# Attention scores: two rows of queries take their blocks of keys in turn

## The chip, the cores and the metric

The kernel runs on one core of a Trainium2 chip. The metric is the device time of one execution in microseconds (us), lower is better. The core has a matrix engine (TensorE, in the rows PE for the matmuls and PEld for the loading of their weights), VectorE (DVE), ScalarE (ACT), GpSimd (POOL) and SyncE (SP), which only issues transfers here. Each engine works through its own instructions in the order in which they were written and waits on semaphores for the others.

## The reference, cut to what matters

One step of a streaming encoder with two layers, for a prompt of 2048 tokens and 8 running streams of 16 tokens. Each layer projects its input to all branches, runs attention A (8 heads of 64, each chunk of 64 tokens sees itself and the 8 chunks before it, with a learned bias), a gated convolution B, and attention C (4 heads with two maps of 32 dimensions, all chunks up to the own one), and projects back. Per head:

```
A:  p = softmax(q k^T / 8 + bias)                      # at most 9 chunks of keys
    out = p v
C:  p1 = softmax(q1 k1^T / sqrt(32)), p2 = softmax(q2 k2^T / sqrt(32))
    out = (p1 - lambda * p2) v                         # two maps, the whole past
```

## The kernel before

The 2048 tokens go through in four segments of 512 (`s` = 0 to 3) for each of the two layers (`l`), which makes eight rounds. Each round is a list of units in `ORDER`, written as letters: P is the projection of a C head and C its attention, K the projection of an A head and A its attention, V, G and O are value, gate and output projections, B the convolution, T a piece of the running streams' attention, N the norm for the next round. Layer 1's last segment has a list of its own.

The functions don't issue instructions, they add them to a `Program`. Its `order` then plays the whole program on five engines with a cost for each instruction and a latency for each pair of engines (`LATENCY`; 127 ns from VectorE to VectorE), and at each step starts the ready instruction that stands earliest in the program. Matmuls of the projections are put back by `LATER` = 350 places, so that they fill what the attention leaves free. The list that comes out is issued as it stands, so that every engine's order is fixed before the kernel runs. Buffers are handed out under a name in the program's order: PSUM bank pair `s` (two banks of 512 columns for all scores), `t` (three banks for transposes), `mm` (two, projections), `o` (one, output), and in SBUF `row` (4 buffers of 2048), `arow` (4 of 640) and `sm` (12 small ones).

Score values are kept negated, so that a row's minimum stands for its maximum. `c_attn` takes a head's four tiles of 128 queries in two pairs. For each tile (`i`) and each of the two maps (`m`), keys come in blocks of up to 512, `s + 1` of them: a matmul into a bank of `s`, then one VectorE instruction that scales, writes the block to a `row`, and takes the running minimum in a column of `mn`. Its starting value (`init`) is the column that the block before has just written. The last block of a row, of 128, 256, 384 or 512 columns, adds the mask of the diagonal. When a map's last block is through, ScalarE takes the exponential of the whole row with the minimum as its bias, and sums it. After both maps VectorE makes the reciprocals and one combined row (`pm[0]`). When a pair has both its rows, TensorE transposes them in blocks of 128 keys, ScalarE and VectorE split each into a high and a low part (`pth`, `ptl`), and TensorE multiplies them by the values.

`a_attn` does the same with one map, up to 640 keys (two blocks of 320 for `s` > 0, one block of 128 to 512 for `s` = 0), two matmuls for each block, a bias that is loaded, an exponential, a reciprocal and a scaling of the row on ScalarE. Its transposes begin with a block of keys that all four tiles use, so that all four rows have to be done.

On the chip an instruction that also writes its minimum shows as two rows, the work itself and a short reading of the accumulator (`READ_ACCUMULATOR`).

Of the kernel before, what the change touches and what calls it, by code (L numbers as in the profile page):

```python
# [13 lines left out]
AF = mybir.ActivationFunctionType  # L14
# [4 lines left out]
P = 128  # L19
# [14 lines left out]
                sm=(12, 8))  # L34
# [273 lines left out]
def trunk(ctx, tc, ins, outs):  # L308
# [4 lines left out]
    pr = Program(tc)  # L313
# [10 lines left out]
    nc = pr  # L324
    sb = pr.tile
# [14 lines left out]
    def mi(shape):  # L340
        return sb("mi", shape)

    def row(shape):
        return sb("row", shape)

    def sm(shape):
        return sb("sm", shape)

    def mm(lhsT, rhs, out, start, stop):
        nc.tensor.matmul(out, lhsT=lhsT, rhs=rhs, start=start, stop=stop)  # L350
# [332 lines left out]
    def k_stack(dst, z):  # L683

        for rep in range(2):
            nc.sync.dma_start(out=R(dst[64 * rep:64 * rep + 64, :, :]).rearrange("p m t -> p (m t)"),
                              in_=bass.AP(z.tensor, z.offset + 64 * 1024, [[1024, 64], [1, 1024]]))
# [51 lines left out]
    def c_rows(s):  # L739

        if s >= 2:
            return [row([P, 2048])[:, 0:2048] for _ in range(2)]
        if s == 1:
            t = row([P, 2, 1024])
            return [t[:, m, :] for m in range(2)]

    def c_attn(l, s, h, q4, k4, v2, on):
        ks, vs = [], []
        for c in range(s):
            kt = sb("ch", [P, 2, 512])  # L750
            k_stack(kt, czs[l, c, h])
            ks.append(kt)
        for c in range(s):
            vt = sb("cv", [P, 4, P])
            nc.sync.dma_start(out=R(vt), in_=cvh[l, c, h])
            vs.append(vt)
        ks.append(k4)
        vs.append(v2)
        for pr in range(2):
            rows = []  # L760
            r1 = sm([P, 2, 2])
            if s == 0:
                both = row([P, 4, 512])
            for ii in range(2):
                i = 2 * pr + ii
                gi = 4 * s + i
                L = P * (gi + 1)
                pm = [both[:, 2 * ii + m, :] for m in range(2)] if s == 0 else c_rows(s)
                sums = sm([P, 2])
                for m in range(2):  # L770
                    mn = sm([P, 4])
                    nch = s + 1
                    for c in range(nch):
                        w = min(512, L - 512 * c)
                        ps = sb("s", [P, 512])
                        mm(q4[:, m, i * P:i * P + P], ks[c][:, m, 0:w], ps[:, 0:w], True, True)
                        o = pm[m][:, 512 * c:512 * c + w]
                        init = BIG if c == 0 else mn[:, c - 1:c]
                        if c < nch - 1:
                            nc.vector.tensor_scalar(out=o, in0=ps[:, 0:w], scalar1=CSC, scalar2=init, op0=ALU.mult,  # L780
                                                    op1=ALU.min, accum_out=mn[:, c:c + 1])
                        else:
                            chunks = lambda ap: ap.rearrange("p (n c) -> p n c", c=64)
                            nc.vector.tensor_tensor_reduce(out=chunks(o), in0=chunks(ps[:, 0:w]),
                                                           in1=mask[:, 8 - w // 64:8].unsqueeze(2).to_broadcast([P, w // 64, 64]),
                                                           scale=CSC, scalar=init, op0=ALU.add, op1=ALU.min, accum_out=mn[:, c:c + 1])
                    nc.scalar.activation(pm[m][:, 0:L], pm[m][:, 0:L], AF.Exp, bias=mn[:, nch - 1:nch], scale=-1.0,
                                         accum_out=sums[:, m:m + 1])
                rr = r1[:, ii, :]
                nc.vector.reciprocal(rr, sums)  # L790
                cc = sm([P, 1])
                nc.vector.scalar_tensor_tensor(out=cc, in0=sums[:, 0:1], scalar=rr[:, 1:2], in1=neglam[l], op0=ALU.mult, op1=ALU.mult)
                nc.vector.scalar_tensor_tensor(out=pm[0][:, 0:L], in0=pm[1][:, 0:L], scalar=cc, in1=pm[0][:, 0:L],
                                               op0=ALU.mult, op1=ALU.add)
                rows.append(pm[0])
            nk = 4 * s + 2 * pr + 2
            po = sb("o", [P, 384])
            pn = po[:, 256:384].rearrange("p (i e) -> p i e", i=2)
            po = po[:, 0:256].rearrange("p (i c) -> p i c", i=2)
            for jj in range(nk // 2):  # L800
                tp = sb("t", [P, 2, 2, P])
                ph, pl = sb("pth", [P, 2, 2, P]), sb("ptl", [P, 2, 2, P])
                last = jj == nk // 2 - 1
                for j2 in range(2):
                    for ii in range(2):
                        if last and j2 == 1 and ii == 0:
                            continue
                        j = 2 * jj + j2
                        nc.tensor.transpose(tp[:, j2, ii, :], rows[ii][:, j * P:j * P + P], ident)
                if last:  # L810
                    split(tp[:, 0], ph[:, 0], pl[:, 0])
                    split(tp[:, 1, 1, :], ph[:, 1, 1, :], pl[:, 1, 1, :])
                else:
                    split(tp, ph, pl)
                for j2 in range(2):
                    j = 2 * jj + j2
                    v = vs[j // 4][:, j % 4, :]
                    lo = 1 if last and j2 == 1 else 0
                    mm(v, ph[:, j2, lo:2, :], po[:, lo:2, :], j == 0, False)
                    mm(v, pl[:, j2, lo:2, :], po[:, lo:2, :], False, last and j2 == 1)  # L820
            o2 = mi([P, P])
            for ii in range(2):
                half, other = slice(64 * ii, 64 * ii + 64), slice(64 - 64 * ii, 128 - 64 * ii)
                nc.scalar.copy(o2[half], po[other, ii, :])
                nc.vector.tensor_tensor(out=o2[half], in0=po[half, ii, :], in1=o2[half], op=ALU.add)
            nc.tensor.transpose(pn.rearrange("p i e -> p (i e)"), o2, ident)
            for ii in range(2):
                nc.scalar.activation(on[:, 2 * pr + ii, h % 2, :], pn[:, ii, :], AF.Copy, scale=r1[:, ii, 0:1])
# [94 lines left out]
    def a_attn(l, s, h, qq, kst, gt):  # L923
# [7 lines left out]
        bt = sb("bias", [P, 640])  # L931
        nc.sync.dma_start(out=bt, in_=nbias[l, h])
        rows = []
        for i in range(4):
            rw = sb("arow", [P, 640])
            rows.append(rw)
            j0 = 512 - P * i if s == 0 else 0
            n = 640 - j0
            cuts = [(j0, 640)] if n <= 512 else [(j0, j0 + n // 2), (j0 + n // 2, 640)]
            mn = sm([P, 2])  # L940
            for ci, (a, b) in enumerate(cuts):
                w = b - a
                ps = sb("s", [P, 512])
                ka = P * i + a
                qs = slice(i * P, i * P + P)
                mm(qq[:, 0, qs], kst[:, ka:ka + w], ps[:, 0:w], True, False)
                mm(qq[:, 1, qs], kst[:, ka:ka + w], ps[:, 0:w], False, True)
                nc.vector.tensor_tensor_reduce(out=rw[:, a:b], in0=ps[:, 0:w], in1=bt[:, a:b], scale=1.0,
                                               scalar=BIG if ci == 0 else mn[:, 0:1], op0=ALU.add, op1=ALU.min,
                                               accum_out=mn[:, ci:ci + 1])  # L950
            nci = len(cuts)
            sums = sm([P, 1])
            pr = rw[:, j0:640]
            nc.scalar.activation(pr, pr, AF.Exp, bias=mn[:, nci - 1:nci], scale=-1.0, accum_out=sums)
            rr = sm([P, 1])
            nc.vector.reciprocal(rr, sums)
            nc.scalar.activation(pr, pr, AF.Copy, scale=rr)
        js = [4, 5, 6, 7] if s == 0 else [3, 4, 2, 1, 0, 5, 6, 7]
        po = sb("o", [P, 512])
        for n, j in enumerate(js):  # L960
# [288 lines left out]
    for n, (l, s) in enumerate(rounds):  # L1249
# [11 lines left out]
        for item in ORDER[s if n + 1 < len(rounds) else NSEG].split():  # L1261
            op, i = item[0], int(item[1:] or 0)
# [125 lines left out]
```

## Time and profile before

| | |
|---|---|
| median of 3 runs | 3255.74 us (3254.12 to 3258.36) |
| profiled execution | 3262.4 us, of which the span from the first to the last instruction is 3260.7 us |
| mean granted clock of TensorE | 0.991 of 2.4 GHz |
| busy | PE 94%, PEld 85%, DVE 71%, ACT 55%, POOL 51% of the span |

All durations and waits below come from the profiled execution. The names in its rows are those of the program's tiles: `s<-kst,qq` is a score matmul of A, `s<-ch,q` and `s<-k,q` are those of C, `arow<-s,bias,sm` and `row<-s,sm` are VectorE's blocks that start from an earlier minimum (without `sm`: first blocks). All lines are L305, where the finished order is issued, so that the tiles' names tell the work.

### The profile page before, as it was taken

How to read it: one execution, taken by the hardware profiler on the slowest of the kernel's cores; microseconds unless marked ns; L12 is line 12 of the kernel's file. 1: busy time of each engine (PE TensorE's matmuls, PEld its weight loads, DVE VectorE, ACT ScalarE, POOL GpSimd, SP SyncE). 2: the span in 40 equal slices, each digit the busy share in tenths (PEclk: the TensorE clock that was granted, in tenths of full speed). 3: DMA queues.
4: the chain of work that ended last, by engine and by line, in shares of the span. 5: the costliest groups of instructions: out<-in, count | busy, mean ns of one | idle time of the engine just before them, and what ended most of it. 6: DMA issues, size and time to landing. Idle time of an engine off the chain costs nothing. (4 is left out here: it accounts for less than half of the span.)

```text
span 3260.7 us, 60379 instructions
## 1 busy us (share of the span) xinstructions
PE 3055.7 (94%) x20416; PEld 2764.5 (85%) x20416; DVE 2326.3 (71%) x5753; ACT 1782.0 (55%) x3817; POOL 1648.2 (51%) x1789
## 2 busy tenths in 40 slices
PE   7999899899999999999999999999899999999998
PEld 7888888788898888987888888888688988889878
DVE  3667778678685866878556576777867858587884
ACT  2654456465473654657445454665555646565652
POOL 5344564445636375453745446444555355744454
PEclk9999999999999999999999999999999999999999
DMA  6665565565655455554575655746666465655543
GB/s 209 206 183 162 162 207 169 178 191 174 199 154 167 139 186 159 161 151 128 189 220 182 179 159 182 212 150 193 213 205 189 139 185 186 190 151 159 175 119 101
DMA packets 438278, 567.51 MB, mean 174 GB/s; under 512 B 88016, under 2 KB 245200, under 8 KB 437968
## 3 DMA queue, kind: packets, MB, share of 16 engines
q1 hardware_dynamic: 437968, 563.65, 57.1%
q8 instruction: 161, 2.64, 0.3%
q14 instruction: 149, 1.22, 0.1%
HBM read 443.67 MB, written 119.84 MB: 173 GB/s over the span
## 5 line engine op out<-in xcount | busy, mean ns | idle before, releaser
L305 POOL TENSOR_SCALAR whi<-w 128x512 fp32r<-128x512 f32 x640 | 455.6, 712 | 1159.3 <-PE mm L305 705.1
L305 POOL TENSOR_TENSOR wlo<-w,whi 128x512 fp32r<-128x512 f32 x640 | 873.3, 1365 | 57.2 <-PE mm L305 8.4
L305 PE MATMUL mm<-whi,ah 128*128 128x256 f32 x2560 | 734.9, 288 | 8.3 <-ACT ah L305 5.9
L305 PE MATMUL mm<-wlo,ah 128*128 128x256 f32 x2560 | 738.0, 289 | 0.3 <-POOL wlo L305 0.2
L305 PE MATMUL mm<-whi,al 128*128 128x256 f32 x2560 | 737.2, 288 | 0.0
L305 PE MATMUL mm<-ah,whi 128*128 128x512 f32 (+2 forms) x1600 | 591.0, 370 | 7.0 <-DVE mi L305 2.3
L305 PE MATMUL mm<-al,whi 128*128 128x512 f32 (+2 forms) x1600 | 587.1, 367 | 0.0
L305 PE MATMUL mm<-ah,wlo 128*128 128x512 f32 (+2 forms) x1600 | 587.0, 368 | 0.0
L305 ACT ACTIVATE arow<-arow,sm 128x640 f32<-128x640 f32 (+4 forms) x560 | 421.1, 768 | 158.0 <-DVE sm L305 154.9
L305 PEld LDWEIGHTS mm<-whi,ah 128*128 128x128 f32 x2560 | 492.2, 193 | 15.4 <-ACT ah L305 6.2
L305 DVE TENSOR_TENSOR ptl<-t,pth 128x512 fp32r<-128x512 f32 (+3 forms) x800 | 400.7, 520 | 137.0 <-ACT pth L305 85.2
L305 PEld LDWEIGHTS mm<-wlo,ah 128*128 128x128 f32 x2560 | 492.9, 193 | 5.6 <-POOL wlo L305 0.7
L305 ACT CAST pth<-t 128x512 fp32r<-128x512 f32 (+3 forms) x800 | 346.3, 453 | 276.3 <-PE t L305 97.3
L305 PEld LDWEIGHTS mm<-whi,al 128*128 128x128 f32 x2560 | 492.9, 193 | 4.5
L305 ACT ACTIVATE row<-row,sm 128x512 f32<-128x512 f32 (+15 forms) x256 | 308.5, 1206 | 192.8 <-DVE sm L305 191.7
L305 PEld LDWEIGHTS mm<-ah,whi 128*128 128x128 f32 x1600 | 303.0, 190 | 39.6 <-POOL whi L305 2.9
L305 PEld LDWEIGHTS mm<-ah,wlo 128*128 128x128 f32 x1600 | 303.2, 190 | 28.8
L305 PEld LDWEIGHTS mm<-al,whi 128*128 128x128 f32 x1600 | 303.8, 190 | 27.9
L305 PE MATMUL t<-ident,arow 128*128 128x128 f32 x1280 | 240.7, 278 | 11.2 <-ACT arow L305 4.8
L305 PE MATMUL t<-ident,row 128*128 128x128 f32 x1360 | 214.3, 279 | 34.6 <-DVE row L305 31.3
L305 DVE SCALAR_TENSOR_TENSOR row<-row,sm,row 128x1024 f32<-128x1024 f32 (+6 forms) x115 | 199.3, 1733 | 50.8 <-POOL sm L305 44.6
L305 PE MATMUL s<-kst,qq 128*128 128x320 f32 (+4 forms) x896 | 219.8, 328 | 16.1 <-DVE sm L305 7.5
(162 smaller groups left out, 5716.6 us busy)
## 6 DMA issues: line engine op xcount, KB each, us to landing
w<-in_w_in SPq DMA_DIRECT2D x512, 256.0 KB, 3.2
w<-in_w_out SPq DMA_DIRECT2D x128, 256.0 KB, 3.1
v2a<-avh SPq DMA_DIRECT2D x112, 256.0 KB, 3.6
ch<-cz SPq DMA_DIRECT2D x96, 256.0 KB, 4.5
bias<-nbias SPq DMA_DIRECT2D x64, 320.0 KB, 3.8
avh<-qq SPq DMA_DIRECT2D x32, 512.0 KB, 3.6
q<-cz SPq DMA_DIRECT2D x64, 256.0 KB, 4.7
k<-cz SPq DMA_DIRECT2D x64, 256.0 KB, 5.9
```

Source lines behind the costliest of these rows:

```text
L305: getattr(engines[i.eng], i.op)(*[real(x) for x in i.a], **{n: real(x) for n, x in i.k.items()})
```

## The change

In C the loop over blocks is now outside and the loop over maps inside: block 0 of map 0, block 0 of map 1, block 1 of map 0 and so on. The two exponentials follow behind all blocks of the tile. In A two tiles of queries are taken together: their first blocks, then their second blocks, then the exponential, reciprocal and scaling of the one and of the other. The instructions, their shapes and their number stay the same, and so do the buffers, `ORDER` and the planner. For segment 0, where each row has one block, only the places in the program change.

```
-                for m in range(2):
-                    mn = sm([P, 4])
-                    nch = s + 1
-                    for c in range(nch):
-                        w = min(512, L - 512 * c)
-                        ps = sb("s", [P, 512])
+                mns = [sm([P, 4]) for _ in range(2)]
+                nch = s + 1
+                for c in range(nch):
+                    w = min(512, L - 512 * c)
+                    for m in range(2):
+                        ps, mn = sb("s", [P, 512]), mns[m]
                         mm(q4[:, m, i * P:i * P + P], ks[c][:, m, 0:w], ps[:, 0:w], True, True)
...
-                    nc.scalar.activation(pm[m][:, 0:L], pm[m][:, 0:L], AF.Exp, bias=mn[:, nch - 1:nch], scale=-1.0,
+                for m in range(2):
+                    nc.scalar.activation(pm[m][:, 0:L], pm[m][:, 0:L], AF.Exp, bias=mns[m][:, nch - 1:nch], scale=-1.0,
                                          accum_out=sums[:, m:m + 1])
...
-        for i in range(4):
-            rw = sb("arow", [P, 640])
...
+        for i in range(0, 4, 2):
+            parts = []
+            for i2 in (i, i + 1):
+                rows.append(sb("arow", [P, 640]))
...
+                mn = sm([P, 2])
+                parts += [(ci, i2, a, b, mn) for ci, (a, b) in enumerate(cuts)]
+            last = {}
+            for ci, i2, a, b, mn in sorted(parts, key=lambda x: x[:2]):
...
+            for i2 in (i, i + 1):
+                sums = sm([P, 1])
+                pr = rows[i2][:, 512 - P * i2 if s == 0 else 0:640]
+                nc.scalar.activation(pr, pr, AF.Exp, bias=last[i2], scale=-1.0, accum_out=sums)
+                rr = sm([P, 1])
+                nc.vector.reciprocal(rr, sums)
+                nc.scalar.activation(pr, pr, AF.Copy, scale=rr)
```

## Rows read from the trace of the kernel before

**Rows 1.** The page's first part: busy us, share of the span, instructions

```profile
PE 3055.7 (94%) x20416; PEld 2764.5 (85%) x20416; DVE 2326.3 (71%) x5753; ACT 1782.0 (55%) x3817; POOL 1648.2 (51%) x1789
```

**Rows 2.** Stretches (segments 1, 3): us, busy PE, PEld, DVE, ACT, POOL; clock, DMA share, GB/s

```profile
440.00:860.00 420.00, 389.60 (x2489) 342.78 (x2489) 317.44 (x782) 242.88 (x524) 212.89 (x230) 0.99 0.62 186
...
1190.00:1610.00 420.00, 405.95 (x2705) 365.53 (x2705) 315.16 (x751) 246.64 (x458) 219.62 (x222) 0.99 0.53 158
```

**Rows 3.** Waits of the matmuls from 100 us on: total us, times, longest

```profile
PE s L305 <- DVE sm L305: 20.6, 33, 1.8
PE o L305 <- DVE ptl L305: 18.3, 26, 2.5
PE t L305 <- DVE row L305: 17.3, 29, 1.6
PE t L305 <- DVE mi L305: 11.9, 12, 3.6
PE o L305 <- DVE v2a L305: 10.7, 8, 4.6
...
PE s L305 <- DVE ptl L305: 6.0, 13, 1.2
PE t L305 <- ACT arow L305: 4.8, 9, 1.4
PE s L305 <- DVE row L305: 4.8, 10, 0.9
```

**Rows 4.** Groups by tile and shape: count, busy us, mean ns of one, idle before

```profile
L305 DVE TENSOR_SCALAR_CACHE_REDUCE row<-s,sm 128x512 f32<-128x512 f32 x192 | 143.3, 746 | 16.0 <-PE s L305 5.6 <-DVE sm L305 0.8
...
L305 DVE CUSTOM_DVE_ANT_0 arow<-s,bias,sm 128x320 f32<-128x320 f32 x192 | 104.7, 545 | 20.4 <-PE s L305 12.6 <-DVE sm L305 0.3
...
L305 DVE CUSTOM_DVE_ANT_1 row<-s,mask,sm 128x512 f32<-128x512 f32 x48 | 35.7, 744 | 1.7 <-PE s L305 0.6
...
L305 DVE CUSTOM_DVE_ANT_1 row<-s,mask,sm 128x128 f32<-128x128 f32 x48 | 16.7, 347 | 7.3 <-PE s L305 4.2 <-DVE row L305 0.8 <-PE t L305 0.3
```

**Rows 5.** VectorE in order of time, a C tile of segment 2: start, us, instruction

```profile
1126.79 0.08 DVE L305 DVE_READ_ACCUMULATOR2_ANT sm<- 128x1 f32 x1
1126.79 1.42 DVE L305 SCALAR_TENSOR_TENSOR row<-row,sm,row 128x1152 f32<-128x1152 f32 x1
...
1129.32 0.09 DVE L305 DVE_READ_ACCUMULATOR row<-s 128x1 f32 x1
1129.53 0.75 DVE L305 TENSOR_SCALAR_CACHE_REDUCE row<-s,sm 128x512 f32<-128x512 f32 x1
```

**Rows 6.** VectorE in order of time, first and last of 156 such pairs

```profile
447.04 0.08 DVE L305 DVE_READ_ACCUMULATOR row<-s 128x1 f32 x1
447.28 0.35 DVE L305 CUSTOM_DVE_ANT_1 row<-s,mask,sm 128x128 f32<-128x128 f32 x1 [0.15 <-DVE row L305]
...
3157.10 0.08 DVE L305 DVE_READ_ACCUMULATOR row<-s,sm 128x1 f32 x1
3157.29 0.75 DVE L305 TENSOR_SCALAR_CACHE_REDUCE row<-s,sm 128x512 f32<-128x512 f32 x1
```

**Rows 7.** All engines in order of time, scores of an A head in segment 3

```profile
1361.30 0.49 DVE L305 CUSTOM_DVE_ANT_0 arow<-s,bias 128x320 f32<-128x320 f32 x1
...
1362.04 0.55 DVE L305 CUSTOM_DVE_ANT_0 arow<-s,bias,sm 128x320 f32<-128x320 f32 x1 [0.24 <-PE s L305]
1362.08 0.46 PE L305 MATMUL s<-kst,qq 128*128 128x320 f32 x2
...
1362.58 0.49 DVE L305 CUSTOM_DVE_ANT_0 arow<-s,bias 128x320 f32<-128x320 f32 x1
```

**Rows 8.** Groups of ScalarE by shape: exponentials of C rows, accumulator reading

```profile
L305 ACT ACTIVATION_READ_ACCUMULATOR row<-row,sm 128x1 f32 x256 | 47.9, 187 | 0.0
...
L305 ACT ACTIVATE row<-row,sm 128x2048 f32<-128x2048 f32 x16 | 32.1, 2007 | 2.1 <-DVE sm L305 2.1
...
L305 ACT ACTIVATE row<-row,sm 128x640 f32<-128x640 f32 x16 | 13.3, 833 | 14.0 <-DVE sm L305 14.0
```

More of the change, by code (lines that the diff above doesn't have):

```diff
@@ L933, in a_attn @@
         rows = []
-        for i in range(4):
-            rw = sb("arow", [P, 640])
[L936 to L941, printed above, removed]
+        for i in range(0, 4, 2):
+            parts = []
+            for i2 in (i, i + 1):
+                rows.append(sb("arow", [P, 640]))
+                j0 = 512 - P * i2 if s == 0 else 0
+                n = 640 - j0
+                cuts = [(j0, 640)] if n <= 512 else [(j0, j0 + n // 2), (j0 + n // 2, 640)]
+                mn = sm([P, 2])
+                parts += [(ci, i2, a, b, mn) for ci, (a, b) in enumerate(cuts)]
+            last = {}
+            for ci, i2, a, b, mn in sorted(parts, key=lambda x: x[:2]):
@@ L942, in a_attn @@
                 w = b - a
                 ps = sb("s", [P, 512])
-                ka = P * i + a
-                qs = slice(i * P, i * P + P)
+                ka = P * i2 + a
+                qs = slice(i2 * P, i2 * P + P)
                 mm(qq[:, 0, qs], kst[:, ka:ka + w], ps[:, 0:w], True, False)
                 mm(qq[:, 1, qs], kst[:, ka:ka + w], ps[:, 0:w], False, True)
-                nc.vector.tensor_tensor_reduce(out=rw[:, a:b], in0=ps[:, 0:w], in1=bt[:, a:b], scale=1.0,
+                nc.vector.tensor_tensor_reduce(out=rows[i2][:, a:b], in0=ps[:, 0:w], in1=bt[:, a:b], scale=1.0,
@@ L949, in a_attn @@
                                                scalar=BIG if ci == 0 else mn[:, 0:1], op0=ALU.add, op1=ALU.min,
                                                accum_out=mn[:, ci:ci + 1])
[L951 to L957, printed above, removed]
+                last[i2] = mn[:, ci:ci + 1]
```

## The prediction

> **What bounds the kernel now.** I read the page's busy shares first. TensorE is at 94% and VectorE at 71% [rows 1]: the reader is to see that time given back on VectorE is worth nothing in itself, only where TensorE stood idle for it. Then busy time by stretches: in segment 1 TensorE is idle 420.0 - 389.6 = 30 us of 420, in segment 3, where C's rows are longest, 14 us [rows 2]. So the scores are densest where there is least idle time to win. Then the waits of the matmuls from 100 us on, past the start [rows 3]: what lies between the change and the end is a score matmul that waits for its bank (`s` on VectorE's `sm` and `row`: 20.6 + 4.8 = 25.4 us in 33 + 10 = 43 waits), a transpose that waits for a finished row (`t` on VectorE's `row`: 17.3 us, 29 waits, the rows of the norms among them, and on `arow`: 4.8 us, 9 waits), and other work of VectorE that came late (`ptl` 18.3 and 6.0, `mi` 11.9, `v2a` 10.7: 46.9 us in 59 waits). Last I read VectorE's instructions in order of time.
>
> **The change, part by part.** No instruction is added or removed and no shape changes, so the 3055.7 us of matmuls [rows 1] stay. No transfer is moved in the program; the planner deals all queues anew, SP's and POOL's too, and I put that in the uncertainty.
>
> *The stall that goes.* A block that starts from the minimum of the block right before it starts 0.21 us behind that block's accumulator reading (1129.32 to 1129.53), while an instruction that doesn't need it starts together with the reading (both at 1126.79) [rows 5]. So 0.21 us is the price of one dependent pair. The blocks that can pay it are 192 middle ones and 4 x 48 last ones of C (the four shapes from 128 to 512) and 192 of A, 576 in all [rows 4]. Most don't pay, since the planner has put other work between: counted along VectorE's timeline, 156 follow with nothing between at that distance, from 447.28 to 3157.29 [rows 6], 116 in C and 40 in A. That is 156 / 576 = 0.27 of them, and 156 x 0.21 = 33 us of VectorE's 2326. The bounds are 0 and 576 x 0.21 = 121 us; I take the count.
>
> Here a rule of the Trainium skill speaks against the change: "VectorE: DVE Perf Modes", section "The DRAIN you can't avoid", says that each operation flushes the pipe whatever follows and that a semaphore between chained operations costs nothing extra. By it the two pairs in [rows 5] would cost the same and the gain below would be zero; the trace doesn't agree, with 0.21 us against 0.00.
>
> *What TensorE gets of it.* A bank is freed 0.21 us earlier where the stall lay just ahead: 43 waits x 0.27 x 0.21 = 2.4 us; the ends are 0 and all 25.4. The other late work of VectorE gets the same share of the same price: 59 x 0.27 x 0.21 = 3.3 us. Together -5.7.
>
> *A gets nothing.* With only two banks the next stall is behind the first. In [rows 7] each A block starts at the end of its own matmuls and the dependent ones wait for PE (0.24 and 0.28 us): two blocks take 1362.58 - 1361.30 = 1.28 us, which is a block (0.49), the two matmuls that refill its bank (0.46) and the signals between them. A dependent pair alone would take 0.49 + 0.55 + 0.21 = 1.25 us. So in a dense run of A the 0.21 us hides behind the refill, and alternating rows leaves 1.28. For C's 0.75 us blocks it hides less, since the other bank's block gives more time to refill.
>
> *What comes later.* In C the exponential of map 0 ran beside map 1's blocks. Now its minimum is ready one block before map 1's, and ScalarE does both exponentials behind the blocks. The tile's end moves by one exponential with its reading, less one last block: the mean exponential over the twelve lengths of segments 1 to 3 (even steps from 640 to 2048) is (2.007 + 0.833) / 2 = 1.42 us, the reading 0.19 [rows 8], the last block (0.744 + 0.347) / 2 = 0.55 [rows 4]: 1.06 us later. Against it stand the stalls that go, on average 4 dependent blocks in a tile (2, 4 or 6) x 116 / 384 x 0.21 = 0.25. Net 0.81 us later per tile, 96 tiles, 77 us of chain. Behind the waiting exponential on ScalarE stand casts of `pth`, for which VectorE and TensorE wait next. It costs nothing where projection matmuls fill TensorE, which the planner deals by the longer chain; if that cover were gone at every present wait for a row it would be 29 x 0.81 = 23.5 us. I take a quarter, 5.9, because TensorE is 97% busy (405.95 of 420) where the rows are longest [rows 2].
>
> In A the first row's exponential waits for the second row's first block, about half of the 1.28 us, 0.64. Its transposes need all four rows, which go one after another through ScalarE. Bounds: 0 and 9 present waits x 0.64 = 5.8 us; a quarter, 1.4, for the same reason.
>
> *Sum:* -2.4 - 3.3 + 5.9 + 1.4 = +1.6 us on the profiled execution's 3262.4. That execution lay 6.7 us above the median of the runs (3255.74), and the forecast is for the median: 3257, no change that a measurement can tell. For this kernel that is 0.2%, 6.5 us: the three runs shown lie 4.2 us apart.
>
> **The rivals.**
> *VectorE's relief reaches further.* Its 33 us lie in the stretches in which it is most loaded, and a matmul that is late once is late for what follows. For it: the five largest waits in [rows 3] are all for VectorE. Against it: TensorE's idle time is least where the blocks are most. If half of the 25.4 us of bank waits and a tenth of the 46.9 us go, with the losses as above, it is -12.7 - 4.7 + 7.3 = -10: 3246. The end is all 25.4 us: 3230.
> *The two exponentials at a tile's end decide.* Place: between a C tile's last block and its combined row. Price 77 us of chain. For it: transposes already wait 29 times for a row. Against: the planner knows the length and has projections left. It is slower by more than 6.5 us as soon as TensorE stands for more than (6.5 + 5.7) / 77 = 16% of it. At 25% it is +19 - 5.7 = +13.5: 3269. All present waits at full price give 23.5: 3279.
> *The wait moves to the banks.* In C, too, VectorE would start from the other map and find its bank not refilled, as A shows [rows 7], so that waits for `sm` become waits for `s`. Then the change doesn't do what it says: the gain is 0, the later rows remain, +7.3: 3263, on the border of what can be told. The Trainium skill's rule above leads to the same time by another way, as there would be no stall to remove.
>
> **How the numbers follow.** The forecast has 0.32, VectorE's relief 0.33, the exponentials 0.22, the banks 0.13 (0.07 no change, 0.06 slower). So faster 0.33, same 0.39, slower 0.28. The forecast's own range is 3250 to 3262. The whole range goes from the far end of the relief, 3255.7 - 25.4 = 3230, to 3255.7 + 23.5 = 3279. A little less than that, 3232 to 3278, leaves out the cases in which one of these is exhausted or in which the new order of all queues adds something of its own; I give them 2 in 10. That order is the cost for which the trace has no row.
>
> **What would show it.** *Stall:* in the profile after, the 156 direct pairs should be nearly gone and what follows an accumulator reading should start with it; VectorE's busy sum should stay near 2326 us. *Banks:* the 25.4 us of `s` on VectorE should fall by a few us; if VectorE's idle time before `row` blocks on "PE s" (5.6 us for the middle ones [rows 4]) rises to several times that, the banks took the stall. *Tail:* two exponentials of C should stand back to back on ScalarE, and `t` on `row` should rise from 17.3 us by 5 or less; by 15 or more it is the second rival. *A:* its two-block period should stay at 1.28 us. I am wrong if waits that have nothing to do with scores (DMA, POOL, projections) change by more than these: then the planner's new order is the cause, and not the stall.

## The result and the profile after

The changed kernel takes 3286.07 us (median of 6 runs, 3279.83 to 3289.91) against 3258.96 us for the kernel before (6 runs, 3254.12 to 3263.32). The ratio is 1.0082, with a 95% interval of 1.0068 to 1.0096: 0.82% slower, some 27 us. Forecast was no change, 3257 us in a range of 3232 to 3278.

The page's first part for the changed kernel (span, then busy us, share, instructions), to be read against [rows 1]:

```profile
span 3286.7 us, 60172 instructions
...
PE 3069.5 (93%) x20416; PEld 2770.8 (84%) x20416; DVE 2313.0 (70%) x5753; ACT 1774.2 (54%) x3817; POOL 1642.8 (50%) x1789
```

The profiled span grew by 3286.7 - 3260.7 = 26.0 us. Of that, 13.8 us is matmul time (3069.5 against 3055.7) for the same 20416 matmuls, which have the same shapes. The other 12.2 us is time in which no matmul ran. VectorE's busy time fell by 13.3 us. The mean granted clock of TensorE is 0.986, before 0.991; how much of the longer matmul time that explains is in the last section.

The waits of the matmuls from 100 us on, as in [rows 3] (total us, times, longest):

```profile
PE t L305 <- DVE row L305: 27.4, 35, 3.4
PE o L305 <- DVE ptl L305: 15.2, 20, 4.9
PE s L305 <- DVE sm L305: 13.3, 24, 1.0
PE t L305 <- DVE mi L305: 13.1, 16, 1.9
PE s L305 <- DVE ptl L305: 10.3, 17, 2.5
PE t L305 <- ACT arow L305: 10.2, 12, 3.0
...
PE s L305 <- DVE row L305: 6.0, 11, 0.9
```

Score matmuls wait less for their banks (20.6 + 4.8 = 25.4 became 13.3 + 6.0 = 19.3 us). Transposes wait more for rows: 17.3 became 27.4 for `row`, 4.8 became 10.2 for `arow`. Read alone, this trace leans to the second rival, the two exponentials at a tile's end, though the 10.1 us more on `row` lie between the prediction's two signs (5 or less for the forecast, 15 or more for the rival). Its sign for the planner's new order doesn't show: summed over all of TensorE's waits from 100 us on, those for POOL went from 29.2 to 25.9 us, those for DMA from 12.4 to 12.7, and those of the projections' matmuls from 9.2 to 11.8. The experiments below don't bear out the exponentials as the cause of the 27 us, and they show that these signs don't tell one cause from the other.

The mechanism itself is there. VectorE and then ScalarE in order of time, a C tile with rows of 1280 keys (start, us, instruction), changed kernel:

```profile
1129.48 0.73 DVE L305 TENSOR_SCALAR_CACHE_REDUCE row<-s,sm 128x512 f32<-128x512 f32 x1
1130.15 0.08 DVE L305 DVE_READ_ACCUMULATOR row<-s,sm 128x1 f32 x1
1130.15 0.47 DVE L305 CUSTOM_DVE_ANT_1 row<-s,mask,sm 128x256 f32<-128x256 f32 x1
1130.55 0.08 DVE L305 DVE_READ_ACCUMULATOR2_ANT sm<- 128x1 f32 x1
1130.73 0.49 DVE L305 CUSTOM_DVE_ANT_1 row<-s,mask,sm 128x256 f32<-128x256 f32 x1
1131.13 0.09 DVE L305 DVE_READ_ACCUMULATOR2_ANT sm<- 128x1 f32 x1
...
1133.96 1.96 DVE L305 SCALAR_TENSOR_TENSOR row<-row,sm,row 128x1280 f32<-128x1280 f32 x1
```

```profile
1130.66 1.37 ACT L305 ACTIVATE row<-row,sm 128x1280 f32<-128x1280 f32 x1 [7.03 <-DVE sm L305]
1131.94 0.18 ACT L305 ACTIVATION_READ_ACCUMULATOR row<-row,sm 128x1 f32 x1
1132.03 1.35 ACT L305 ACTIVATE row<-row,sm 128x1280 f32<-128x1280 f32 x1
```

The last block of map 0 starts together with the accumulator reading of map 1's block (both at 1130.15), where a dependent one started 0.21 us later in [rows 5]. Counted as for [rows 6], 16 direct pairs are left of 156. And the exponentials stand back to back (1130.66 and 1132.03): from the last block's reading to the combined row it is 1133.96 - 1131.13 = 2.83 us. The same step of a 1280-key tile of the kernel before, on VectorE:

```profile
1130.84 0.08 DVE L305 DVE_READ_ACCUMULATOR2_ANT sm<- 128x1 f32 x1
...
1132.90 1.55 DVE L305 SCALAR_TENSOR_TENSOR row<-row,sm,row 128x1280 f32<-128x1280 f32 x1
```

There it was 1132.90 - 1130.84 = 2.06 us, so this tile's end came 0.77 us later. That step leaves out the stalls that go, so it stands against the prediction's 1.06 us and not against its net 0.81. By the prediction's working this tile would give 1.37 + 0.18 - 0.47 = 1.08 us; the second exponential starts at the end of the first (1132.03), while the accumulator reading is still going on, so the reading adds nothing to the chain here, and from the last block of map 0 to that of map 1 it is 1131.13 - 1130.55 = 0.58 us instead of 0.47.

What became of VectorE's stall is in the groups by tile and shape of the changed kernel (count, busy, mean ns, idle before):

```profile
L305 DVE TENSOR_SCALAR_CACHE_REDUCE row<-s,sm 128x512 f32<-128x512 f32 x192 | 140.9, 745 | 16.3 <-PE s L305 13.6
...
L305 DVE CUSTOM_DVE_ANT_0 arow<-s,bias,sm 128x320 f32<-128x320 f32 x192 | 103.2, 545 | 16.5 <-PE s L305 15.4
```

Against [rows 4], the wait of C's middle blocks for their score matmul rose from 5.6 to 13.6 us and that of A's second blocks from 12.6 to 15.4: part of the stall is now a wait for the banks, more in C than I had thought. In front of C's middle blocks nothing was won at all: their idle time as a whole is 16.3 us, before 16.0. For A's second blocks it fell from 20.4 to 16.5. Where A's blocks follow each other with nothing between, two take 1.43 us in the median (31 cases), before 1.36 (24 cases), so A's period did not get shorter, as forecast.

### The profile page after: what moved, and what is told of

Its sections match the earlier page's. It is cut to its first block, busy times and chain, and to the rows that moved or that the text cites. A ratio compares the mean times of both kernels' runs of the same rounds, so it can differ in the third digit from the quotient of the medians.

```text
span 3286.7 us, 60172 instructions
## 1 busy us (share of the span) xinstructions
PE 3069.5 (93%) x20416; PEld 2770.8 (84%) x20416; DVE 2313.0 (70%) x5753; ACT 1774.2 (54%) x3817; POOL 1642.8 (50%) x1789
## 5 line engine op out<-in xcount | busy, mean ns | idle before, releaser
L305 POOL TENSOR_TENSOR wlo<-w,whi 128x512 fp32r<-128x512 f32 x640 | 869.5, 1359 | 61.2 <-PE mm L305 11.8
L305 PEld LDWEIGHTS mm<-whi,ah 128*128 128x128 f32 x2560 | 491.9, 193 | 21.7 <-ACT ah L305 8.0
L305 PE MATMUL t<-ident,arow 128*128 128x128 f32 x1280 | 239.1, 280 | 16.1 <-ACT arow L305 10.2
```

The costliest lines, as they stand in the source:

```text
L305: getattr(engines[i.eng], i.op)(*[real(x) for x in i.a], **{n: real(x) for n, x in i.k.items()})
```

## Where the time was lost

POOL converts 640 pieces of weights in both kernels; counted in the order of the trace, their starts are milestones. Up to the 281st the changed kernel was 3.7 us ahead (1430.7 against 1434.4 us). It lost 9.1 us from the 281st to the 321st, around the end of segment 3 of layer 0 (15 by the 301st, then 6 back), 9.4 us from the 441st to the 461st, in segment 1 of layer 1, 6 us from the 521st to the 561st (8 won, then 14 lost) and 11.2 us from the 581st to the 621st, in segment 3 of layer 1. Where the planner puts a conversion moves its milestone, so that a step which the next one takes back is not time lost.

The first and the last of these stretches hold 20 of the 26 us, and the traces of the experiments below have the same milestones. There the unchanged kernel, written out by the planner in four other orders (71, 72, 69 and 73 in the table below), lost 23, 17, 17 and 4 us against the kernel before, and the changed kernel in the orders with these numbers 19, 16, 13 and 19. So the kernel before is the fastest of all at these two places, and most of its other orders lose there without the change what the changed kernel loses.

The stretch from the 441st to the 461st holds about the same matmuls in both. First the kernel before, then the changed one (stretch: us, busy us and count of PE, PEld, DVE, ACT, POOL; granted clock, DMA share, GB/s):

```profile
2257.80:2373.20 115.40, 101.64 (x589) 85.44 (x588) 94.32 (x235) 67.82 (x145) 57.86 (x66) 0.96 0.67 209
```

```profile
2263.50:2388.30 124.80, 104.05 (x577) 86.46 (x575) 97.20 (x228) 68.76 (x148) 64.33 (x73) 0.92 0.61 198
```

Twelve matmuls fewer kept TensorE busy 2.4 us longer, at a clock of 0.92 against 0.96, and it was idle 124.80 - 104.05 = 20.8 us against 13.8. The Trainium skill ("Perfetto Trace Analysis", section "Matmul Optimizations") says that the matrix engine scales its power with use and that matmuls should run back to back; the trace agrees as far as the clock goes, with the 0.92. What it was idle for there, in the changed kernel (waits of the matmuls, 2263 to 2390 us):

```profile
PE s L305 <- DVE ptl L305: 4.7, 4, 2.5
PE s L305 <- POOL sm L305: 3.7, 1, 3.7
PE t L305 <- DVE row L305: 3.3, 2, 1.7
PE s L305 <- DVE qq L305: 3.3, 1, 3.3
```

Only one of these four kinds, 3.3 of 15.0 us, is a transpose that waits for a row. The waits for `ptl` and for POOL's `sm` are mostly those of the running streams' scores (`s<-ptl,qq`, `s<-kst`), which the change doesn't touch; the one for `qq` is a score matmul of C (`s<-ch,q`). In the kernel before, the largest wait of this stretch is another one, 7.0 us of the streams for `v2a`. Of the kinds that the prediction had named as signs of the planner's new order (DMA, POOL, projections) only POOL's 3.7 us is among them.

## The experiments

Four theories. *Tail*: both exponentials stand behind a C tile's last block and TensorE has nothing else left at the ends of segments. *A*: the pairs of A do the harm. *Banks*: map 1's early blocks hold a bank while their row isn't free. *Deal*: any edit makes the planner write out another order of the whole program, and the kernel before has a good one. All ratios are to the kernel before, measured beside each experiment.

**Each part alone.** `e1_c_only` has the new `c_attn` and the old `a_attn`, `e2_a_only` the reverse:

```
 e1:  c_attn as in the change:  for c in range(nch): ... for m in range(2): ...
      a_attn as before:         for i in range(4): ...
 e2:  c_attn as before, a_attn as in the change
```

> Only C's blocks alternate, A is as before. The measured change is +27 us. Theory 'tail' (both exponentials of a C tile stand behind its last block, and TensorE has nothing else left at the ends of segments): +20 to +30 us, transposes wait for C rows some 10 us more than the 17.3 us of before. Theory 'A' (the first row's exponential of each pair of A waits for another block): under +8 us. Theory 'deal' (any new order of all queues costs about as much): somewhere from 0 to +30, with no tie to waits for rows.

> Only A's tiles alternate, C is as before. Tail: within 7 us of before. A: +15 us or more, transposes wait for arow some 10 us instead of 4.8. Deal: from 0 to +30.

C alone: 3273.37 us, 1.0049 (1.0031 to 1.0068). A alone: 3255.86 us, 1.0001 (0.9987 to 1.0016). So in these orders A alone costs nothing, C alone 0.5%, some 17 us, and both together 0.8%, which is more than the sum. 'Tail' had 20 to 30 us for C alone. Its waits came nearly as it said: transposes waited 25.1 us for `row`, 7.8 more than before. But score matmuls waited 25.0 us for `sm`, more than the 20.6 of before, though C's blocks alternate:

```profile
PE t L305 <- DVE row L305: 25.1, 31, 3.0
PE s L305 <- DVE sm L305: 25.0, 32, 4.4
```

With A alone, the transposes' wait for `arow` was 8.0 us, where theory 'A' had some 10.

**The tail without the alternation.** `e4_tail` moves only the last blocks together, in segments 2 and 3:

```
+                blocks = [(c, m) for m in range(2) for c in range(nch)]
+                if s > 1:
+                    blocks = [x for x in blocks if x[0] < nch - 1] + [(nch - 1, 0), (nch - 1, 1)]
+                for c, m in blocks:
```

> C in segments 2 and 3: all blocks of map 0 but the last, all of map 1 but the last, then the last of map 0 and the last of map 1; A and segment 1 as before. The exponentials stand behind the last blocks as in the changed kernel, but most blocks still follow their predecessor directly, and map 1's first block doesn't ask for its row early. Tail: +12 to +25 us, most of the loss. Theory 'banks' (map 1's first block holds one of the two banks while its row is not free): within 7 us of before.

3260.41 us, 1.0003 (0.9990 to 1.0016): no loss in this order with the exponentials at the tile's end of segments 2 and 3, where 'tail' had 12 us or more. The transposes' wait for rows rose as in the changed kernel, by 8.5 us, and the time did not:

```profile
PE t L305 <- DVE row L305: 25.8, 32, 3.4
```

**A control that changes no chain.** `e3_maps_swapped` is the kernel before with the maps in the other order:

```
-                for m in range(2):
+                for m in (1, 0):
                     mn = sm([P, 4])
```

> The kernel before with map 1's blocks ahead of map 0's in C: no chain changes its length, only names and buffers change places. It is the control for the planner's new deal. Tail and A: within 7 us of before. Deal: 10 us or more away from before.

3286.27 us, 1.0086 (1.0065 to 1.0106): as much as the whole change, with both exponentials where they were. Its waits, too, look like those of the changed kernel, though no block alternates:

```profile
PE t L305 <- DVE row L305: 26.2, 35, 2.2
...
PE s L305 <- DVE sm L305: 13.9, 26, 1.1
```

It isn't a perfect control, since the first map then asks for the row buffer that comes free later. So I took one that touches the kernel's work nowhere.

**The same kernels in other orders.** The planner's booking of a VectorE instruction has a fixed part of 70 ns. One nanosecond there changes no instruction, no dependency and no buffer count, only what the planner writes out. I did it to both kernels:

```
-            return 70 + n / (0.96 if slow else 1.92) + ...
+            return 71 + n / (0.96 if slow else 1.92) + ...     # d1, d2; 72 in d3, d4; 69 in d5, d6; 73 in d7, d8
```

> The kernel before, but the planner books every VectorE instruction at 1 ns more (71 for 70 ns of fixed cost). No instruction and no dependency of the kernel changes, only the order that the planner writes out. Theory 'deal' (before has a lucky order and any other costs 0 to 30 us by where TensorE falls to half its clock): 8 us or more from before, slower rather than faster. Theory 'chain' (the change's own dependencies make the loss): within 7 us of before.

> The changed kernel with the same 1 ns in the planner. Deal: anywhere from 0 to +30 us over before, 8 us or more away from the changed kernel's 3286. Chain: within 8 us of 3286.

> The kernel before with 2 ns more in the planner's booking of VectorE: a third order of the same work. Deal: different from before and from the 1 ns version by 8 us or more in at least one case. Chain: within 7 us of before.

> The changed kernel with 2 ns more in the planner's booking of VectorE. Deal: the two changed kernels with 1 and 2 ns and the two kernels before with 1 and 2 ns have means within 8 us of each other. Chain: the changed ones lie some 25 us above the others.

> The kernel before with the planner booking VectorE at 1 ns less (69). A fourth order of the same work. Deal (the orders decide, the change is worth less than they scatter): 5 to 35 us over the kernel before. Chain (the change costs some 25 us by itself and the orders nothing) has fallen with the 1 ns version, which lost 33 us without the change.

> The changed kernel with 1 ns less. Deal: 5 to 35 us over the kernel before, not ordered against its partner. Rival 'the change gains under other orders' (so far 9 us less than its partner in the mean of the 1 and 2 ns pairs): below its partner by 5 to 15 us.

> The kernel before with 3 ns more in the planner's booking of VectorE. Deal: 5 to 35 us over the kernel before.

> The changed kernel with 3 ns more. Deal: 5 to 35 us over the kernel before, in either order against its partner. Rival 'the change gains under other orders': below its partner by 5 to 15 us. In all changed kernels the score matmuls' waits for banks should stand below those of all unchanged ones (13 to 17 against 21 to 26 us so far), and the transposes' waits for rows some 3 us above.

| planner's fixed part | kernel before | changed kernel |
|---|---|---|
| 70 (as given) | 1 | 1.0082 (1.0068 to 1.0096) |
| 71 | 1.0102 (1.0082 to 1.0121) | 1.0054 (1.0037 to 1.0071) |
| 72 | 1.0035 (1.0020 to 1.0049) | 1.0027 (1.0015 to 1.0039) |
| 69 | 1.0055 (1.0039 to 1.0070) | 1.0036 (1.0025 to 1.0048) |
| 73 | 0.9988 (0.9976 to 1.0000) | 1.0018 (1.0002 to 1.0035) |
| mean of the five | 1.0036 | 1.0043 |

One nanosecond in the plan costs the kernel before 1.0%, more than the change did. Over five orders the unchanged kernel lies from 0.9988 to 1.0102, the changed one from 1.0018 to 1.0082; in three of five pairs the changed one has the lower ratio, in two of these (72 and 69) with intervals that overlap. The five differences (+0.82, -0.48, -0.08, -0.19, +0.30%) have a mean of +0.07% and a standard deviation of 0.50. The standard error of the mean is about 0.2%, and a 95% interval from five values is about 0.6% to either side: -0.55 to +0.70%. The rival that the change gains under other orders is not borne out: in the last two pairs it was once 0.2% ahead (some 6 us, as the rival said) and once 0.3% behind. Two forecasts of 'deal' missed: the means of the 71 and 72 pairs lie 0.28%, 9 us, apart, where it had 8 at most, and the kernel before at 73 lies 0.1% under the one at 70, where it had 5 to 35 us above.

What all five orders of the change have in common shows in the waits from 100 us on, in us, in the order of the table:

| wait of the matmuls | five orders of before, mean | five orders of the change, mean |
|---|---|---|
| `s` on VectorE's `sm` | 20.6, 21.6, 25.5, 19.9, 24.3: 22.4 | 13.3, 16.0, 16.9, 16.1, 15.3: 15.5 |
| `s` on VectorE's `row` | 4.8, 11.5, 6.6, 5.3, 6.0: 6.8 | 6.0, 7.6, 6.8, 6.1, 6.9: 6.7 |
| `t` on VectorE's `row` | 17.3, 24.0, 20.2, 27.7, 19.1: 21.7 | 27.4, 19.7, 23.4, 23.7, 25.1: 23.9 |
| `t` on ScalarE's `arow` | 4.8, 4.0, 7.6, 8.2, 10.5: 7.0 | 10.2, 5.4, 6.6, 8.1, 12.2: 8.5 |

The three lines of the views that answer for the pair at 72, of the unchanged kernel and then of the changed one:

```profile
PE s L305 <- DVE sm L305: 25.5, 31, 1.9
PE t L305 <- DVE row L305: 20.2, 33, 2.1
PE t L305 <- ACT arow L305: 7.6, 13, 1.4
```

```profile
PE t L305 <- DVE row L305: 23.4, 30, 3.5
PE s L305 <- DVE sm L305: 16.9, 31, 1.1
...
PE t L305 <- ACT arow L305: 6.6, 8, 1.6
```

In the first line of the table no value of the one kind reaches the other's: bank waits fall by 6.9 us. That the alternation does it isn't shown. The swapped maps have 13.9 us with no block alternating, and C alone 25.0 with C's blocks alternating, so another order moves this wait as far as the change does. The waits for rows rise by 2.2 and 1.5 us, less than they scatter. Net that is -3.3 us, which the five times can't tell from nothing.

On VectorE, the waits of its `row` blocks for score matmuls have a mean of 62.8 us over the five orders of the change (54.5 to 69.3), before 48.8 (44.7 to 57.1); those of `arow` are 50.9 and 50.3. By these means some 14 of the 33 us of stall became waits for the banks, in C. With C alone it is 52.9, inside what the unchanged kernel does.

With scatter of this size the runs e1 to e4 say less than their intervals seem to. Each interval is that of one order. C alone (1.0049), the swapped maps (1.0086) and the moved last blocks (1.0003) all lie within what the unchanged kernel does for a nanosecond. They speak against a tail that must cost 12 us, and against A alone as the cause, and no more. The banks theory for the swapped maps was not followed up.

## Why the prediction was wrong

- **The matmul time** was wrong: "the 3055.7 us of matmuls [rows 1] stay" left nothing for it, and it grew by 13.8 us for the same matmuls, half of the 26.0 us of the profiled span. In its other orders the unchanged kernel has 3058.9 to 3068.5 us of it.
- **The stall** was right as a count: 0.21 us for a dependent pair, 156 pairs of which 16 are left, and the next block starts with the reading. The Trainium skill ("VectorE: DVE Perf Modes", section "The DRAIN you can't avoid") says that a semaphore between chained operations costs nothing extra, measured on a chain of copies. It is not what this trace shows for a block that reads the minimum of the one before it, with 0.21 us.
- **What TensorE gets** can't be told: forecast were 2.4 us of bank waits, and the mean over five orders is 6.9 less, but another order alone moves this wait as far. The 3.3 us for other late work can't be seen in the scatter.
- **The banks** took more in C than forecast: middle blocks wait 13.6 instead of 5.6 us for their matmuls, and their idle time as a whole did not fall. That is the third rival's mechanism in part; its time, 3263, was far from the one measured. A gained nothing measurable, alone 1.0001.
- **What comes later** was right in kind and somewhat too large: 0.77 us in the tile shown, where the prediction's working gives 1.08, since it counted the reading and took the last block too short. Transposes wait 2.2 us more for `row` and 1.5 for `arow` on average, forecast 5.9 and 1.4; both are less than the orders scatter.
- **The sum** of +1.6 us is near the mean over five orders, +0.07% (2 us), but that mean is known to no better than about 20 us to either side, and two of its terms are off or can't be told, so that it comes so near is luck; and it is not what the one pair of kernels shows. The step that failed is the one that put "the planner deals all queues anew" into the uncertainty: "the cost for which the trace has no row" was left to the 2 cases in 10 outside a range that was made of waits for scores and rows alone. It is the largest term: five orders of the same kernel lie up to 37 us apart (0.9988 to 1.0102). The first order stands second of the five, so that a change that is worth nothing was likelier to lose than to win: the other four orders of the unchanged kernel lie 0.45% above it in the mean, the five of the changed one 0.43%.
- **The second rival**, slower by the exponentials, would have named the sign and part of the size (3269) for a reason that is not the one shown.

Shown is that a new order by itself moves the unchanged kernel by as much as the 27 us, with losses at the same places, and that over five orders the two kernels can't be told apart. By the means, 0.45 of the 0.82% is the good order of the kernel before, and the rest the changed kernel's own order, the worst of its five. How the 27 us really divide between the order and the change's own cost is not shown: the five pairs leave the change anything from -0.55 to +0.70%. Which pieces of an order make the ends of segments run dry, and why the first order avoids it, stays open.

## What to carry to other kernels

Where a planner writes the whole order, an edit is two changes, its own and a new order. Measure the second by itself with a perturbation that touches no work, a nanosecond in a cost, and judge the edit over several orders of both kernels. Hold a wait that seems to be the edit's own against a control, too: here the bank waits fell in all five orders of the change, and as far in a kernel in which only the maps were swapped.

## What was not expected of the hardware

The changed kernel needed 13.8 us more for the same 20416 matmuls at a mean clock of 0.986 instead of 0.991, about as much as it stood idle longer (12.2 us), and in the stretch shown 0.92 instead of 0.96. So half of the loss stands in the profile as matmul time and not as a wait.

In that stretch TensorE waited 3.68 us, up to 2327.61, and 3.27 us, up to 2341.12. The granted clock of 2326.0 to 2336.2 and of 2339.6 to 2346.4 is 0.50, the lower level (1.2 GHz), and from 2346.4 to 2356.0 it is 1.00 (2.4 GHz). The same matmul at either level:

```profile
2342.11 0.63 PE L305 MATMUL mm<-ah,whi 128*128 128x512 f32 x1
...
2348.99 0.39 PE L305 MATMUL mm<-ah,whi 128*128 128x512 f32 x1
```

Over the whole profile the clock stood at 0.50 for 93.7 us, with matmuls running in 71.6 of them; before, for 60.3 us with 51.5. An estimate from these: if that work takes half the time at the higher level, the clock explains (71.6 - 51.5) / 2 = 10 of the 13.8 us. The rest stays open, and it isn't small everywhere: with the fixed part at 71 the unchanged kernel has 12.1 us more matmul time (3067.8) at a mean clock of 0.990.
